# Four small edits to a one-core decoder block: later work on loads, a third row buffer, one low part on another engine, a moved constant

## The chip, the core and the metric

The kernel runs on one core of one Trainium2 chip. The metric is device time in microseconds (us) of one execution, the median over the runs shown. A profile of one further execution, taken by the hardware profiler, is read beside it.

## What is computed

One decoder layer on a sequence of 1024 tokens with 1024 channels, in float32:

```python
mod = silu(c) @ w_ada + b_ada
shift, scale, gate = split(mod, 3)
h = rms_norm(x, norm_gain) * (1 + scale) + shift
q, k, v, z_a, u, z_b, m_a, m_b = split(h @ w_in, ...)          # each (1024, 1024)
attn = stick_breaking_attention(q, k, v)                       # 16 heads of 64
p_a = (attn * silu(z_a)) @ w_branch_a
p_b = (multiscale_causal_pool(u, pool_w, pool_scale) * silu(z_b)) @ w_branch_b
out = (sigmoid(m_a) * p_a + sigmoid(m_b) * p_b) @ w_out
return rms_norm(x + gate * out, final_gain)
```

In the attention each weight is sigmoid(z) times the product of (1 - sigmoid(z)) over the keys between, under a strictly causal mask. The pooling takes means over trailing windows of 2, 4, 8 and 16 tokens, one window for each quarter of the channels.

## The kernel before, in words

**Split products.** Every large product is made of three matmuls in a reduced float32 format. A weight or an activation is held as a high part (a rounded copy, made by ScalarE or VectorE) and a low part (the value minus its high part, made by VectorE or GpSimd), and high x high, high x low and low x high are summed in PSUM (`mm3`, L162). `split` (L110) makes both parts, the high one at L119 or L123 and the low one at L114; `load_w` (L125) loads a tile of 128 x 1024 weights and calls it. The engines that make the two parts are its last arguments.

**Stages.** The work goes in this order: the modulation, the normalised input `hT` and the first half of u (up to L536); the second half of u (L571); the values v (L579 to L601); z_b with the pooled branch (L604 to L621); the product with w_branch_b (L630 to L641); attention together with the projections k, q, z_a, m_a, m_b (L649 to L940); and last the product with w_branch_a, the sum of the two branches, the product with w_out and the final norm (L943 to L1026).

**Low parts ahead of time.** The attention stage reads 40 tiles of `w_in` in the order of `tiles` (L131). The first `PLAIN` = 8 are split where they are loaded, by `load_parts` (L152): high part on ScalarE, low part on GpSimd. With index 0 the tile of the first pair's keys, 1 its queries, 2 its z_a, and 3 the second pair's keys, index 4 is the second pair's queries. For the 32 others `make_lo` (L138) runs in the earlier stages: it loads the tile (L147), makes the high part on ScalarE (L148), the low part on VectorE in place (L149), and stores it to DRAM in `wl_d` (L150). In the values' stage it has three buffers for the raw tile and one for the high part, and each step makes `LO_V[sb]` tiles, 0 or 1.

**Values' stage.** Two halves of eight steps. A step is 24 matmuls of 512 columns into one of two PSUM banks, a high part of the result on ScalarE (L593), a low part on VectorE (L594), a store (L595), then `make_lo`, and in steps 1, 4, 7 and 10 one `make_d` (L544), which loads a tile of u and computes window mean minus token on VectorE (L553 to L560). The weights of the second half of the stage are loaded and split in the same stage (`load_wv`, L565).

**Attention stage.** Its order on TensorE is written out and kept (`pinned`, L95): logits of blocks of 128 queries (L795), then two sigmoids on ScalarE into `om` and `be` (L797, L798), a mask on the diagonal block of each on GpSimd (L802), a running product on VectorE (L804), and a product of the two (L805), after which `om`, which has two buffers, is free. Later the weights are turned on TensorE with the identity `ident` as moving operand (L107), split again (L823, L824), and multiplied with the values (L835). Between these steps come pieces of the projections.

**Last stage.** For each half of the tokens and each of eight row blocks j, rows of sigmoid(m_a), sigmoid(m_b) and p_b are loaded from DRAM into `s_`, `m_` and `b_`, each with two buffers (L963 to L968). `m_` is multiplied with `b_` (L969), 24 matmuls `pa` run, VectorE multiplies the result by `s_` and frees the PSUM bank (L976), adds (L977), and splits the sum into `mhl` (L978, its low part at L114). These matmuls alternate in two PSUM banks with one another and lie among those of `o`, the product with w_out (L1000).

**What sets the order.** Outside the stretch that is pinned, the order of each engine's instructions is not the order of the program text: a planner that simulates a timeline sorts them, within the limits of the buffers. Each engine then executes its own list strictly in order, waiting where it must. Loads and stores are issued by SyncE's queue (SP), some stores by ScalarE's.

**Memory.** `const` holds the identity (512 bytes in each partition), a tile of ones of the same size, and small vectors; after it comes `big`, with `hT` and later `wo`, and then `wts`, the buffers for weights.

Of the kernel before, what the change touches and what calls it, by code (L numbers as in the profile page):

```python
# [9 lines left out]
F32 = mybir.dt.float32  # L10
F32R = mybir.dt.float32r
# [4 lines left out]
P = 128  # L16
# [18 lines left out]


PLAIN = 8
LO_V = (1, 0, 1, 1, 0, 1, 1, 0)
LO_ZB = (0, 1, 0, 1, 0, 1, 0, 1)
LO_PB = (1, 1, 1, 1, 1, 1, 2, 2)  # L40
# [9 lines left out]
WINDOWS = (2, 4, 8, 16)  # L50
# [5 lines left out]
def block_kernel(ctx, tc, a, out):  # L56
# [3 lines left out]
    def pool(name, **kw):  # L60
        return tc.tile_pool(name=name, bufs=1, reuse_waits="tile", **kw)

    const = ctx.enter_context(pool("const"))
    big = ctx.enter_context(pool("big"))
    wts = ctx.enter_context(pool("wts"))
    dram = ctx.enter_context(tc.tile_pool(name="dram", bufs=1, space=bass.MemoryType.DRAM))
    psp = ctx.enter_context(tc.tile_pool(name="psp", bufs=2, space=PSUM))
# [10 lines left out]
    u_d = dram.tile([KB, P, S], F32, name="u_d")  # L78
    wl_d = dram.tile([5 * KB, P, D], F32, name="wl_d")

    ident = const.tile([P, P], F32, name="ident")
    make_identity(nc, ident)
    ones = const.tile([P, P], F32, name="ones")
    gp.memset(ones, 1.0)
    mhalf = const.tile([P, 8], F32, name="mhalf")
    gp.memset(mhalf, -0.5)
# [48 lines left out]
    tiles += gates  # L135
    early_lo = iter(range(PLAIN, len(tiles)))

    def make_lo(pl, n, tag=None, bufs=3):  # L138

        for _ in range(n):  # L140
            i = next(early_lo)
            if tag:
                raw, hi = (pl.tile([P, D], t_, tag=tag, bufs=5, name=f"l{i}_{n_}") for n_, t_ in (("raw", F32), ("hi", F32R)))
            else:
                raw = pl.tile([P, D], F32, tag="lraw", bufs=bufs, name=f"l{i}_raw")
                hi = pl.tile([P, D], F32R, tag="lhi", bufs=1, name=f"l{i}_hi")
            nc.sync.dma_start(raw, a["w_in"][tiles[i]])  # L147
            act.copy(hi, raw)  # L148
            v.tensor_sub(raw.bitcast(F32R), raw, hi.bitcast(F32))  # L149
            nc.sync.dma_start(wl_d[i], raw)  # L150

    def load_parts(i, name):  # L152
        if i < PLAIN:
            return load_w(a["w_in"][tiles[i]], name, act, gp)
        raw = wts.tile([P, KB, P], F32, tag="raw", bufs=2, name=name + "_raw")
        nc.sync.dma_start(raw.rearrange("p k c -> p (k c)"), a["w_in"][tiles[i]])
        hl = wts.tile([P, 2, KB, P], F32R, tag="whl", bufs=2, name=name)
        nc.sync.dma_start(hl[:, 1].rearrange("p k c -> p (k c)").bitcast(F32), wl_d[i])
        act.copy(hl[:, 0], raw)
        return hl[:, 0], hl[:, 1]  # L160
# [380 lines left out]
        gp.memset(invn[:, j:j + 1], 1.0 / (16 - j))  # L541
    dhls = {}

    def make_d(j):  # L544
        win = WINDOWS[j // 2]
        u = dif.tile([P, S + 16], F32, tag="u", bufs=2, name=f"u{j}")
        v.memset(u[:, S:], 0.0)
        nc.sync.dma_start(u[:, :S], u_d[j])
        cur, n, step = u, S + 16, 1
        while step < win:  # L550
            nxt = dif.tile([P, S + 16], F32, tag="win", bufs=2, name=f"win{j}_{step}")
            n -= step
            v.tensor_add(nxt[:, :n], cur[:, :n], cur[:, step:step + n])  # L553
            cur, step = nxt, 2 * step
        t0 = S - win + 1
        d = dif.tile([P, S], F32, tag="d", bufs=5, name=f"d{j}")
        v.scalar_tensor_tensor(d[:, :t0], cur[:, :t0], 1.0 / win, u[:, :t0], ALU.mult, ALU.subtract)
        tl = dif.tile([P, 16], F32, tag="tl", bufs=2, name=f"tl{j}")
        v.tensor_mul(tl[:, :win - 1], cur[:, t0:S], invn[:, 16 - win + 1:])
        v.tensor_sub(d[:, t0:], tl[:, :win - 1], u[:, t0:S])  # L560
        dhls[j] = d


    with pool("vp") as vp:
        def load_wv(hf, k2):  # L565
            raw = wts.tile([P, 2, 512], F32, tag="raw", bufs=2, name=f"wv{hf}_{k2}_raw")
            nc.sync.dma_start(raw.rearrange("p k c -> p (k c)"), a["w_v"][hf, k2])
            return split(raw, [P, 2, 512], vp, "wv", 6, act, v, f"wv{hf}_{k2}")

        wv = [[load_wv(0, k2) for k2 in range(4)]]  # L570
        for i in reversed(range(KB)):  # L571
            ps = bank("pj", f"u{i}_1")
            mm3(ps, whl[i], h, range(KB), hmov(1))
            use[i](1, ps)
            make_lo(vp, 1)
        early.close()
        diffs = ExitStack()
        dif = diffs.enter_context(pool("dif", side="right"))
        for hf in range(2):  # L579
            if hf == 0:  # L580
                wv.append([load_wv(1, k2) for k2 in range(4)])
            for sb in range(8):
                ss = slice(sb * P, (sb + 1) * P)
                ps = bank("pj", f"v{sb}_{hf}")
                for kb in range(KB):
                    hh, hl = h_hi[:, kb, ss], h_lo[:, kb, ss]
                    wh, wl = (w[:, kb % 2] for w in wv[hf][kb // 2])
                    for n, (l, w) in enumerate(((hh, wh), (hh, wl), (hl, wh))):
                        mm(ps, l, w, start=kb == 0 and n == 0, stop=kb == KB - 1 and n == 2)

                vo = dif.tile([P, 8, 2, HD], F32R, tag="vo", bufs=3, name=f"vo{sb}_{hf}")
                pv = ps.rearrange("p (h d) -> p h d", d=HD)
                act.copy(vo[:, :, 0], pv)  # L593
                v.tensor_sub(vo[:, :, 1], pv, vo[:, :, 0].bitcast(F32))  # L594
                nc.sync.dma_start(  # L595
                    v_d[4 * hf:4 * hf + 4, :, sb].rearrange("n p c -> p n c"),
                    vo.rearrange("p (n h) i d -> p n (h i d)", h=2).bitcast(F32),
                )
                make_lo(vp, LO_V[sb])
                if 8 * hf + sb in DIFFS:  # L600
                    make_d(DIFFS[8 * hf + sb])  # L601


    with pool("pb") as pb:  # L604
        gb = pb.tile([P, 2, KB, S], F32R, name="gb")
        for j in range(KB):
            if j not in dhls:
                make_d(j)
            zs = [pb.tile([P, 512], F32, tag="zs", bufs=3, name=f"zs{j}_{sh}") for sh in range(2)]

            def silu(sh, ps):
                z, sl = zs[sh], slice(sh * 512, sh * 512 + 512)
                act.activation(z, ps, AF.Sigmoid)
                v.tensor_mul(z, ps, z)
                v.scalar_tensor_tensor(z, dhls[j][:, sl], psc_v[:, j:j + 1], z, ALU.mult, ALU.mult)
                act.copy(gb[:, 0, j, sl], z)
                v.tensor_sub(gb[:, 1, j, sl], z, gb[:, 0, j, sl].bitcast(F32))

            project(CZB + j, f"wzb{j}", silu, act, v)
            make_lo(pb, LO_ZB[j], bufs=2)  # L620
            del dhls[j]  # L621

        sg, gjunk = (dif.tile([P, S + 16], F32, tag="u", bufs=2, name=n)[:, :D] for n in ("sg", "gjunk"))
        nc.sync.dma_start(sg, a["c_row"].broadcast_to([P, D]))
        act.activation(gjunk, sg, AF.Sigmoid)
        v.tensor_mul(sg, sg, gjunk)
        gate = pb.tile([P, KB], F32, name="gate")
        bias = pb.tile([P, KB], F32, name="gbias")
        nc.sync.dma_start(bias, a["b_gate"])
        for j in range(KB):  # L630
            sm = [pb.tile([P, 512], F32, tag="zs", bufs=3, name=f"sm{j}_{sh}") for sh in range(2)]
            whl = load_w(a["w_branch_b"][j], f"wb{j}", v, gp)
            wg = wts.tile([P, D], F32, tag="raw", bufs=2, name=f"wg{j}")
            nc.sync.dma_start(wg, a["w_gate"][j])
            v.scalar_tensor_tensor(gjunk, wg, 1.0, sg, ALU.mult, ALU.mult, accum_out=gate[:, j:j + 1])
            for sh in range(2):
                ps = bank("pj", f"pb{j}_{sh}")
                mm3(ps, whl, (gb[:, 0], gb[:, 1]), range(KB), hmov(sh))
                act.copy(sm[sh], ps)
                nc.sync.dma_start(pb_d[j][:, sh * 512:sh * 512 + 512], sm[sh])  # L640
            make_lo(dif, LO_PB[j], "d")  # L641

        v.tensor_add(gate, gate, bias)
        nc.sync.dma_start(g_d[0].rearrange("(k p) -> p k", p=P), gate)
# [298 lines left out]
    with pool("fin") as fin:  # L943
# [14 lines left out]
        for sh in range(2):  # L958
            sl = slice(sh * 512, sh * 512 + 512)
            ms = []  # L960
            for j in range(KB):
                whl = load_w(a["w_branch_a"][j], f"wa{sh}_{j}", act, v)
                s_ = fin.tile([P, 512], F32, tag="s_", bufs=2, name=f"s{sh}_{j}")  # L963
                nc.sync.dma_start(s_, sa_d[j][:, sl])
                m_ = fin.tile([P, 512], F32, tag="m_", bufs=2, name=f"m{sh}_{j}")
                nc.sync.dma_start(m_, sb_d[j][:, sl])
                b_ = fin.tile([P, 512], F32, tag="b_", bufs=2, name=f"b{sh}_{j}")
                nc.sync.dma_start(b_, pb_d[j][:, sl])  # L968
                v.tensor_mul(m_, m_, b_)  # L969
                ps = bank("pj", f"pa{sh}_{j}")  # L970
# [111 lines left out]
```

## Time and profile before

| what | value |
|---|---|
| median of 3 runs | 1212.78 us (1212.56 to 1213.09) |
| the profiled execution's own time | 1212.4 us |
| span of its trace, first to last instruction | 1210.4 us |
| TensorE busy in the span | 1199.6 us, 99% |
| VectorE, ScalarE, GpSimd busy | 63%, 45%, 16% |
| mean granted TensorE clock | 0.999 of full speed |

PE is TensorE's matmuls, PEld its weight loads, DVE is VectorE, ACT is ScalarE, POOL is GpSimd, SP is SyncE; a q behind an engine's name means its queue, which issues transfers. Busy times of PE rest on modelled ends of matmuls, so that the distance between the starts of matmuls is a better measure of their pace than the duration of one.

### The profile page before, as it was taken

How to read it: one execution, taken by the hardware profiler on the slowest of the kernel's cores; microseconds unless marked ns; L12 is line 12 of the kernel's file. 1: busy time of each engine (PE TensorE's matmuls, PEld its weight loads, DVE VectorE, ACT ScalarE, POOL GpSimd, SP SyncE). 2: the span in 40 equal slices, each digit the busy share in tenths (PEclk: the TensorE clock that was granted, in tenths of full speed). 3: DMA queues.
4: the chain of work that ended last, by engine and by line, in shares of the span. 5: the costliest groups of instructions: out<-in, count | busy, mean ns of one | idle time of the engine just before them, and what ended most of it. 6: DMA issues, size and time to landing. Idle time of an engine off the chain costs nothing.

```text
span 1210.4 us, 16174 instructions
## 1 busy us (share of the span) xinstructions
PE 1199.6 (99%) x5746; PEld 1000.1 (83%) x5746; DVE 757.9 (63%) x1049; ACT 540.6 (45%) x1008; POOL 193.8 (16%) x361
## 2 busy tenths in 40 slices
PE   8999999999999999999999999999999999999997
PEld 7888888888888888888888888888888888888886
DVE  6764482677410277767768677776777763785643
ACT  5564341334211265665556655655655653232211
POOL 1000000001222343212212122231211310000001
PEclk9999999999999999999999999999999999999999
DMA  9649994626846632442635325353343236984622
GB/s 361 255 168 339 326 383 167 214 82 230 317 148 117 179 92 75 133 121 78 170 109 157 113 80 153 109 158 115 106 132 102 96 126 211 315 275 168 218 65 84
DMA packets 81955, 207.13 MB, mean 171 GB/s; under 512 B 10450, under 2 KB 23890, under 8 KB 79699
## 3 DMA queue, kind: packets, MB, share of 16 engines
q1 hardware_dynamic: 73666, 191.23, 49.2%
q10 hardware_dynamic: 8208, 14.88, 3.3%
q8 instruction: 45, 0.74, 0.2%
q14 instruction: 36, 0.29, 0.1%
HBM read 138.96 MB, written 50.34 MB: 156 GB/s over the span
## 4 chain that ended last, share of the span: by engine, by line
PE 93%; DVE 2%; DMA 2%; issue 1%; ACT 0%; POOL 0%; SPq 0%; POOLq 0%; DVEq 0%; ACTq 0%
PE p L99 36%; PE pb L99 7%; PE wzb L99 7%; PE v L99 7%; PE o L99 6%; PE av L99 6%; PE z L99 6%; PE wt L99 5%; PE pa L99 5%; PE u L99 5%; PE ua L99 3%; PE wm L99 1%; DMA m<-sb_d 1%; DMA out_y<-y 0%; DMA praw<-in_pool_w 0%
## 5 line engine op out<-in xcount | busy, mean ns | idle before, releaser
L99 PE MATMUL p<-hT,w 128*128 128x512 f32 x1920 | 480.9, 392 | 0.0
L99 PEld LDWEIGHTS p<-hT,w 128*128 128x128 f32 x1920 | 354.8, 188 | 68.6
L804 DVE TENSOR_TENSOR_SCAN om<-om 128x512 f32<-128x512 f32 (+7 forms) x128 | 175.4, 1370 | 50.0 <-ACT om L797 41.5
L824 DVE TENSOR_TENSOR wt<-wt,wt 128x512 fp32r<-128x512 f32 (+1 forms) x160 | 100.5, 628 | 93.7 <-ACT wt L823 93.1
L823 ACT CAST wt<-wt 128x512 fp32r<-128x512 f32 (+1 forms) x160 | 87.5, 547 | 130.2 <-PE wt L99 129.7
L797 ACT ACTIVATE om<-z 128x512 f32<-128x512 f32 (+2 forms) x192 | 94.9, 494 | 77.2 <-PE z L99 52.2
L802 POOL TENSOR_SCALAR_AFFINE_SELECT om<-om 128x128 f32<-128x128 f32 x128 | 50.9, 397 | 364.3 <-ACT om L797 344.0
L99 PE MATMUL av<-wt,vv 128*128 128x512 f32 x320 | 106.0, 412 | 0.0
L99 DVE TENSOR_TENSOR be<-be,om 128x511 f32<-128x511 f32 (+7 forms) x128 | 95.8, 758 | 0.3
L798 ACT ACTIVATE be<-z 128x512 f32<-128x512 f32 (+2 forms) x192 | 94.2, 491 | 0.0
L99 PE MATMUL pa<-ga,wa 128*128 128x512 f32 x384 | 89.9, 390 | 0.3 <-DVE s L976 0.2
L99 PEld LDWEIGHTS wt<-ident,be 128*128 128x128 f32 x576 | 72.7, 140 | 20.9
L99 PE MATMUL o<-wo,mhl 128*128 128x512 f32 (+1 forms) x408 | 89.6, 377 | 0.0
L99 PE MATMUL wt<-ident,be 128*128 128x128 f32 x576 | 88.7, 272 | 0.0
L99 PE MATMUL v<-wv,hT 128*128 128x512 f32 x384 | 87.2, 389 | 0.0
L99 PE MATMUL wzb<-hT,wzb 128*128 128x512 f32 x384 | 87.2, 389 | 0.0
L99 PE MATMUL pb<-gb,wb 128*128 128x512 f32 x384 | 87.2, 389 | 0.0
L99 PEld LDWEIGHTS o<-wo,mhl 128*128 128x128 f32 x408 | 73.5, 188 | 14.1
L99 PEld LDWEIGHTS pa<-ga,wa 128*128 128x128 f32 x384 | 71.9, 188 | 15.9 <-issue 0.6
L99 PEld LDWEIGHTS v<-wv,hT 128*128 128x128 f32 x384 | 72.1, 188 | 14.9
L99 PEld LDWEIGHTS wzb<-hT,wzb 128*128 128x128 f32 x384 | 72.1, 188 | 14.9
L99 PEld LDWEIGHTS pb<-gb,wb 128*128 128x128 f32 x384 | 72.1, 188 | 14.9
(129 smaller groups left out, 1374.2 us busy)
## 6 DMA issues: line engine op xcount, KB each, us to landing
w_raw<-in_w_in SPq DMA_DIRECT2D x40, 512.0 KB, 4.8
l_raw<-in_w_in SPq DMA_DIRECT2D x32, 512.0 KB, 5.1
wl_d<-l_raw SPq DMA_DIRECT2D x32, 512.0 KB, 5.8
w<-wl_d SPq DMA_DIRECT2D x32, 512.0 KB, 3.9
v_d<-vo SPq DMA_DIRECT2D x16, 512.0 KB, 4.8
vv<-v_d SPq DMA_DIRECT2D x8, 1024.0 KB, 5.5
wa_raw<-in_w_branch_a SPq DMA_DIRECT2D x16, 512.0 KB, 4.8
wa<-in_w_mod SPq DMA_DIRECT2D x7, 1024.0 KB, 6.5
```

The lines of the kernel that those rows point to most:

```text
L99: ins = op(*args, **kw)
L797: act.activation(om[:, b0:b0 + n], zp[:, :n], AF.Sigmoid, scale=-0.125)
L798: act.activation(be[:, b0:b0 + n], zp[:, :n], AF.Sigmoid, scale=0.125)
L802: gp.affine_select(out=tl[:, :P], in_=tl[:, :P], pattern=[[1, P]], compare_op=ALU.is_gt, fill=fill, base=0, channel_multiplier=-1)
L804: v.tensor_tensor_scan(om[:, :W], om[:, :W], om[:, :W], 1.0, ALU.mult, ALU.min)
L823: act.copy(wt[:, 0, :off], pt[:, :off])
L824: v.tensor_sub(wt[:, 1, :off], pt[:, :off], wt[:, 0, :off].bitcast(F32))
```

## The change

A tile of the values' stage that `make_lo` has loaded is worked on (high part, low part, store) one step later than it is loaded, and so is the computation of `make_d` behind its load of u. The low part of weight tile 4 of the attention stage moves from GpSimd to VectorE. `s_`, `m_` and `b_` get three buffers each. The identity and the ones move from `const` to a pool of their own behind `big`.

```diff
+MASKED = 4
...
     big = ctx.enter_context(pool("big"))
+    idp = ctx.enter_context(pool("idp"))
     wts = ctx.enter_context(pool("wts"))
...
-    ident = const.tile([P, P], F32, name="ident")
+    ident = idp.tile([P, P], F32, name="ident")
     make_identity(nc, ident)
-    ones = const.tile([P, P], F32, name="ones")
+    ones = idp.tile([P, P], F32, name="ones")
...
-    def make_lo(pl, n, tag=None, bufs=3):
+    def make_lo(pl, n, tag=None, bufs=3, later=False):
+        rest = []
         for _ in range(n):
...
             nc.sync.dma_start(raw, a["w_in"][tiles[i]])
-            act.copy(hi, raw)
-            v.tensor_sub(raw.bitcast(F32R), raw, hi.bitcast(F32))
-            nc.sync.dma_start(wl_d[i], raw)
+            def low(i=i, raw=raw, hi=hi):
+                act.copy(hi, raw)
+                v.tensor_sub(raw.bitcast(F32R), raw, hi.bitcast(F32))
+                nc.sync.dma_start(wl_d[i], raw)
+            if later:
+                rest.append(low)
+            else:
+                low()
+        return rest
...
-            return load_w(a["w_in"][tiles[i]], name, act, gp)
+            return load_w(a["w_in"][tiles[i]], name, act, v if i == MASKED else gp)
...
-    def make_d(j):
-        win = WINDOWS[j // 2]
+    def load_u(j):
         u = dif.tile([P, S + 16], F32, tag="u", bufs=2, name=f"u{j}")
         v.memset(u[:, S:], 0.0)
         nc.sync.dma_start(u[:, :S], u_d[j])
+        return u
+
+    def make_d(j, u):
+        win = WINDOWS[j // 2]
...
-                make_lo(vp, LO_V[sb])
+                now, todo = todo, make_lo(vp, LO_V[sb], later=True)
                 if 8 * hf + sb in DIFFS:
-                    make_d(DIFFS[8 * hf + sb])
+                    j = DIFFS[8 * hf + sb]
+                    todo.append(lambda j=j, u=load_u(j): make_d(j, u))
+                for f in now:
+                    f()
...
-                s_ = fin.tile([P, 512], F32, tag="s_", bufs=2, name=f"s{sh}_{j}")
+                s_ = fin.tile([P, 512], F32, tag="s_", bufs=3, name=f"s{sh}_{j}")
...
-                m_ = fin.tile([P, 512], F32, tag="m_", bufs=2, name=f"m{sh}_{j}")
+                m_ = fin.tile([P, 512], F32, tag="m_", bufs=3, name=f"m{sh}_{j}")
...
-                b_ = fin.tile([P, 512], F32, tag="b_", bufs=2, name=f"b{sh}_{j}")
+                b_ = fin.tile([P, 512], F32, tag="b_", bufs=3, name=f"b{sh}_{j}")
```

## Rows read from the trace of the kernel before

**Rows 1.** The page's first two parts: TensorE's busy time, and its granted clock in 40 slices.

```profile
PE 1199.6 (99%) x5746; PEld 1000.1 (83%) x5746; DVE 757.9 (63%) x1049; ACT 540.6 (45%) x1008; POOL 193.8 (16%) x361
...
PEclk9999999999999999999999999999999999999999
```

**Rows 2.** TensorE's waits over the span: total us, times, longest.

```profile
PE idle L99 <- POOL x L230: 1.6, 1, 1.6
...
PE z L99 <- ACT be L798: 0.4, 1, 0.4
PE pa L99 <- DVE s L976: 0.2, 1, 0.2
```

**Rows 3.** Busy time by stretches: us, PE, PEld, DVE, ACT, POOL, clock, DMA share, GB/s.

```profile
0.00:30.00 30.00, 26.16 (x118) 21.40 (x119) 18.07 (x33) 17.27 (x30) 4.37 (x32) 1.00 0.93 361
...
150.00:180.00 30.00, 30.00 (x134) 24.86 (x133) 25.85 (x33) 12.46 (x16) 0.00 (x0) 1.00 1.02 379
```

**Rows 4.** The chain that ended last, in order of time: start us, us, what.

```profile
79.84 48.47 PE u L99 x212
128.31 87.04 PE v L99 x384
215.35 87.04 PE wzb L99 x384
...
1102.37 21.77 PE o L99 x96
```

**Rows 5.** Timeline of the first masks: start us, us, engine, line, what, idle before.

```profile
425.42 1.23 POOL L802 TENSOR_SCALAR_AFFINE_SELECT be<-be 128x128 f32<-128x128 f32 x1
...
426.65 0.51 ACT L797 ACTIVATE om<-z 128x384 f32<-128x384 f32 x1
426.85 2.40 POOL L114 TENSOR_TENSOR w<-w_raw,w 128x1024 fp32r<-128x1024 f32 x1 [0.20 <-ACT w L119]
...
429.21 0.29 POOL L802 TENSOR_SCALAR_AFFINE_SELECT om<-om 128x128 f32<-128x128 f32 x1
...
429.53 1.02 DVE L804 TENSOR_TENSOR_SCAN om<-om 128x384 f32<-128x384 f32 x1 [2.39 <-POOL om L802]
...
430.46 1.54 PE L99 MATMUL p<-hT,w 128*128 128x512 f32 x6
431.25 0.60 ACT L797 ACTIVATE om<-z 128x512 f32<-128x512 f32 x1 [3.71 <-DVE be L99]
...
432.39 0.50 PE L99 MATMUL z<-kh,q 128*128 128x512 f32 x1 [0.38 <-ACT be L798]
...
439.60 0.59 ACT L692 CAST kh<-p 128x512 fp32r<-128x512 f32 x1 [1.16 <-PE p L99]
```

**Rows 6.** Instructions by line and shape: the same low part on VectorE in the last stage.

```profile
L114 DVE TENSOR_TENSOR wa<-wa_raw,wa 128x1024 fp32r<-128x1024 f32 x16 | 19.5, 1218 | 14.3 <-ACT wa L119 14.3
```

**Rows 7.** Timeline of the last stage, around the two waits of its matmuls.

```profile
1127.37 4.86 PEld L99 LDWEIGHTS pa<-ga,wa 128*128 128x128 f32 x22 [0.49 <-DVE wa L114]
...
1146.77 10.59 PE L99 MATMUL pa<-ga,wa 128*128 128x512 f32 x46
...
1153.03 0.32 SPq L966 DMA_DIRECT2D m<-sb_d  x1
1156.13 0.69 DVE L969 TENSOR_TENSOR m<-m,b 128x512 f32<-128x512 f32 x1 [3.12 <-DMA m<-sb_d]
1156.74 0.68 DVE L976 TENSOR_TENSOR s<-pa,s 128x512 f32<-128x512 f32 x1
...
1157.57 0.70 PE L99 MATMUL pa<-ga,wa 128*128 128x512 f32 x2 [0.21 <-DVE s L976]
```

**Rows 8.** Timeline of VectorE in the values' stage: a d, and the last low of wv.

```profile
153.84 1.23 DVE L553 TENSOR_TENSOR win<-win 128x1037 f32<-128x1037 f32 x1
...
156.12 1.22 DVE L557 SCALAR_TENSOR_TENSOR d<-win,u 128x1021 f32<-128x1021 f32 x1
...
172.06 1.22 DVE L114 TENSOR_TENSOR wv<-wv_raw,wv 128x1024 fp32r<-128x1024 f32 x1
```

More of the change, by code (lines that the diff above doesn't have):

```diff
@@ L577, in block_kernel @@
         diffs = ExitStack()
+        todo = []
         dif = diffs.enter_context(pool("dif", side="right"))
@@ L598, in block_kernel @@
                 )
-                make_lo(vp, LO_V[sb])
+                now, todo = todo, make_lo(vp, LO_V[sb], later=True)
                 if 8 * hf + sb in DIFFS:
-                    make_d(DIFFS[8 * hf + sb])
+                    j = DIFFS[8 * hf + sb]
+                    todo.append(lambda j=j, u=load_u(j): make_d(j, u))
+                for f in now:
+                    f()
+        assert not todo
     with pool("pb") as pb:
@@ L607, in block_kernel @@
             if j not in dhls:
-                make_d(j)
+                make_d(j, load_u(j))
             zs = [pb.tile([P, 512], F32, tag="zs", bufs=3, name=f"zs{j}_{sh}") for sh in range(2)]
```

## The prediction, made before the changed kernel was run

> **What bounds the kernel now.** I read the busy times first: TensorE is busy for 1199.6 of 1210.4 us, at its upper clock level, 2.4 GHz, in nearly every slice [rows 1]. So a part of the change can gain only where TensorE waits, and the next view is the list of its waits. Of six, the first and three more lie in the first stretch of 30 us, where it is busy for 26.16 us only [rows 2, 3]; no part of the change touches those. Two are left: 0.4 us at logits z, waiting for a sigmoid, and 0.2 us at pa, waiting for the step that frees a PSUM bank [rows 2].
>
> A modelled end hides part of a wait, so I measure pace by starts. The chain of waits gives it: 384 matmuls of v in 87.04 us and 384 of wzb in the same time are 0.2267 us each [rows 4]. The values' stage, where most lines of the change are, is then TensorE back to back from 128.31 to 215.35 us. That is the first thing to see: nothing can be gained there. For the two waits I use the timeline around each.
>
> **First masks, low part to VectorE.** Tile 4's low part runs on GpSimd for 2.40 us from 426.85 us. The mask of an `om` whose sigmoid began at 426.65 and took 0.51 us (ready at 427.16) has to queue behind it until 429.21; the running product on VectorE, idle for 2.39 us until then, starts at 429.53; `om` comes free and ScalarE goes on at 431.25; TensorE's next z starts at 432.39 [rows 5]. Six p started at 430.46 and would have been done at 430.46 + 6 x 0.2267 = 431.82. So 0.57 us are lost here.
>
> The change adds to VectorE one instruction of 1.22 us, the price of the same shape there [rows 6]. VectorE's gap runs from 427.14 to 429.53 [rows 5], and the high part ends just before 426.85, where GpSimd started on it, so the low part fits: 427.14 + 1.22 = 428.36. What then comes first decides the shift. If the mask runs beside it, the running product starts at 428.36, 1.17 us earlier; if the planner puts it before the low part, it can start about 427.5, 2.0 us earlier. Both cover 0.57. The weights have time: TensorE needs them after the second pair's keys, whose last copy starts at 439.60 [rows 5], some 10 us later. If VectorE's gap is not there because ScalarE or the planner has moved things, the low part costs at most its 1.22 us in that chain. I take -0.57.
>
> Here a row bears on the margin. A mask took 1.23 us beside a running product, where another takes 0.29 [rows 5]. The Trainium skill's SBUF — State Buffer, section Who interferes with whom, says that a VectorE instruction with two SBUF inputs and a GpSimd instruction that reads SBUF shut each other out, the second for the whole of the first. The trace agrees with it at that row (1.23 against 0.29 us). By that rule the mask would wait for the low part and the sum would still be -0.57, with a thinner margin. In numbers of the trace alone: a mask that starts at 428.36 and takes 0.29 lets the running product start about 428.7, 0.8 us earlier instead of 1.17, which leaves 0.26 over 0.57. One more delay of 0.3 us in that chain and part of the wait comes back; this is why I give the case without a gain below more than a token chance.
>
> What is late next? No wait of TensorE stands in the list between this one and the last stage, so up to 0.57 us of advance should be kept; a new wait of the same size is the other bound, 0.
>
> **Third buffers at the end.** 46 pa start at 1146.77 and end at 1146.77 + 46 x 0.2267 = 1157.20; the next start at 1157.57, 0.37 us late [rows 7]. The bank was freed by L976 at 1156.74, which stood on VectorE behind L969 at 1156.13, and that had idled for 3.12 us for the load of `m_`, issued at 1153.03 when its buffer came free [rows 7]. A third buffer frees the place one row block earlier, 24 x 0.2267 = 5.44 us, so that the load goes out about 1147.6 and lands about 1150.7; L969 then waits for nothing, and L976 follows 3 us earlier. -0.37. The other loss, 0.49 us at 1127.37, is a weight's low part (L114) [rows 7], which no buffer of rows touches; I leave it, as the bound below.
>
> The cost: 3 x 2 KB in each partition, and on SP the loads of `s_`, `m_`, `b_` may stand a block earlier, ahead of weight loads. Since their place is then free, they don't hold the queue longer; 0, at worst a slip like the 0.49 already there.
>
> **Values' stage.** Nothing is added or removed: each load, high part, low part, store and d has the same duration, a step (5.44 us) later. ScalarE and VectorE should wait less inside a step, which TensorE does not notice. On SP a step's store now stands behind the next step's load, and a raw buffer is held a step longer; three buffers against at most one tile a step allow it. The last tile's work falls under the first wzb, whose matmuls take 87.04 us without a gap [rows 4]. I take 0. What hides this work is slack on VectorE, and that is thin in one place: from 150 to 180 us it is busy for 25.85 of 30 us [rows 3]. More on that below.
>
> **Identity and ones.** No instruction more or less; `big` moves down by 1 KB. The trace can bound what a place is worth: v, wzb and o read operands in different places and run at 87.04/384 = 0.2267 and 21.77/96 = 0.2268 us [rows 4]. Some 3100 matmuls read `hT`; at 0.1 ns each that is 0.3 us either way. I take 0.
>
> **Sum.** -0.57 - 0.37 = -0.94 us. The profiled execution took 1212.4 us with a span of 1210.4, so it would be 1211.5; the median of the runs is 0.4 above it, 1212.78, so I forecast **1211.8**. About 0.2% (2.4 us) is what a measurement can tell from no change here, so this counts as none.
>
> **Rivals.**
> *More waits go* (0.17). Every edit lets the planner sort anew, and it may clear what I left: the 0.49 us at 1127, and in the second half of u 48.47 - 212 x 0.2267 = 0.41 us [rows 4]. With both, 1210.9; with 0.3 from the place, 1210.6. Past 1210.4 there is little in the trace after the first 30 us that could still be gained.
> *The change doesn't do what it says* (0.20). The planner sorts instructions outside the pinned stretch, so "a step later" may leave the order as it is, and one of the two waits may come back by the margins above. 1212.2 to 1212.8; for it speaks that the gap at the masks is a matter of tenths, against it that both waits are traced to the very instruction the change moves or frees.
> *VectorE becomes late in the values' stage* (0.13), the one that ends slower. The last low part of the second half's weights ends at 172.06 + 1.22 = 173.28 us [rows 8]. The second half starts at 128.31 + 192 x 0.2267 = 171.83 and needs that weight after 18 matmuls, at 175.9: 2.6 us of margin. Held work that now stands ahead of it costs 1.2 us for a low part, and for a d of window 4 two sums of 1.23, one of 1.22 and small ones, about 4.0 [rows 8]. One of each, 5.2, overruns by 2.6: 1214.4. Two d's and a low part, 9.2, by 6.6: 1218.4. It decides from 2.6 us ahead of that low part. For it speaks the busy VectorE of that stretch; against it, that the planner sees this due time.
>
> **Chances and range.** The forecast has 0.50, the rivals 0.17, 0.20 and 0.13. Faster by over 0.2% (under 1210.4) is a third of the first rival, 0.06; slower by over 0.2% (over 1215.2) most of the last, 0.10; within, 0.84. The range leaves out those tails: 1210.3, which takes in the low bounds, to 1214.0, which takes in no gain at all, the 1.22 us of a low part in the chain, and little of the last rival.
>
> **What would show it.** In the profile after: a DVE L114 `w` of about 1.22 us near 427 us and no POOL one there; the running product before 428.8; the p and z starts near 432 without a hole; seven POOL L114 `w` in place of eight. At the end: no idle of L969 for `m_` near 1156, and L976 right behind its pa. In the values' stage 384 v in 87.04 us as before; a higher number, or a wait of v for wv in TensorE's list, means the last rival. A changed pace of 0.2267, or transposes that take longer, would mean that the identity's place counts, and I would be wrong there. A time under 1210 would show that TensorE's lost time was more than these waits.

## The result, and the profile after

The changed kernel took 1216.22 us (median of 8 executions, 1215.54 to 1217.81), the kernel before 1212.92 (median of 8 in the same session, 1212.18 to 1214.39). The ratio is 1.0029, interval 1.0019 to 1.004: slower by 3.3 us, outside the forecast range, whose upper end was 1214.0. The profiled execution took 1215.54 us with a span of 1213.7, so 3.3 us more span than before.

The change moved line numbers: the matmul helper is now L103 (L99 before), the low part L118 (L114), the high part on ScalarE L123 (L119), the product with `s_` L998 (L976), the sum L999 (L977), the scaling of y L1041 (L1019).

The page's busy time and clock, to be held against [rows 1]:

```profile
PE 1199.5 (99%) x5746; PEld 999.7 (82%) x5746; DVE 759.9 (63%) x1050; ACT 541.8 (45%) x1008; POOL 194.3 (16%) x360
...
PEclk9999999999999999999999999999999999999999
```

TensorE is busy for the same time, at the same clock level, 2.4 GHz. So most of the 3.3 us are waiting, and the list of TensorE's waits says where (total us, times, longest):

```profile
PE pa L103 <- DVE wa L118: 3.7, 2, 2.2
PE idle L103 <- POOL x L243: 1.6, 1, 1.6
PE ua L103 <- ACT hT L103: 1.1, 1, 1.1
PE ua L103 <- DVE wg L103: 1.0, 1, 1.0
PE wm L103 <- DMA praw<-in_pool_w: 0.7, 1, 0.7
```

Against [rows 2] the two waits that the prediction worked on, z on `be` and pa on `s`, are gone. In their place stand two of pa for the low part of a weight tile, longest 2.2 us. The busy times by stretch show where (us, PE, PEld, DVE, ACT, POOL, clock, DMA share, GB/s), the first two rows answering to [rows 3]:

```profile
0.00:30.00 30.00, 25.65 (x118) 20.89 (x119) 17.99 (x33) 17.30 (x30) 4.38 (x32) 1.00 0.93 357
150.00:180.00 30.00, 30.00 (x134) 24.85 (x133) 25.74 (x33) 11.53 (x14) 0.00 (x0) 1.00 1.00 363
420.00:450.00 30.00, 30.00 (x149) 25.14 (x148) 25.49 (x29) 17.87 (x36) 10.20 (x17) 1.00 0.32 79
1020.00:1050.00 30.00, 28.54 (x126) 23.30 (x125) 14.39 (x20) 6.34 (x7) 0.00 (x0) 1.00 0.87 317
1110.00:1140.00 30.00, 27.76 (x123) 22.65 (x122) 15.21 (x23) 5.93 (x11) 1.92 (x4) 1.00 0.47 166
```

The values' stage and the first masks are full; two stretches of the last stage are not. The chain says the same of the pace (start us, us, what), against [rows 4]:

```profile
128.40 87.04 PE v L103 x384
215.44 87.04 PE wzb L103 x384
...
1103.77 21.76 PE o L103 x96
```

**The first hole.** Timelines of ScalarE, VectorE and TensorE near 1046 (start us, us, engine, line, what, idle before):

```profile
1040.57 1.05 ACT L123 CAST wa<-wa_raw 128x1024 fp32r<-128x1024 f32 x1 [5.25 <-DMA wa_raw<-in_w_branch_a]
...
1043.51 0.69 DVE L118 TENSOR_TENSOR mhl<-m,mhl 128x512 fp32r<-128x512 f32 x1
1045.14 0.69 DVE L998 TENSOR_TENSOR s<-pa,s 128x512 f32<-128x512 f32 x1 [0.95 <-PE pa L103]
1045.75 1.22 DVE L118 TENSOR_TENSOR wa<-wa_raw,wa 128x1024 fp32r<-128x1024 f32 x1
...
1047.02 2.35 PE L103 MATMUL pa<-ga,wa 128*128 128x512 f32 x9 [1.46 <-DVE wa L118]
```

The high part of tile 3 is ready at 1041.62, and VectorE is idle from about 1044.2. It does not make the low part, since its next entry is the product with `s_` of row block 2, which needs the pa that TensorE finishes only at 1045.1. Behind it the low part comes too late: the matmuls start 1.851 us apart instead of 0.227, a loss of 1.62. Before, the same low part ran at 1043.05, ahead of that product:

```profile
1043.05 1.22 DVE L114 TENSOR_TENSOR wa<-wa_raw,wa 128x1024 fp32r<-128x1024 f32 x1
...
1050.54 0.68 DVE L976 TENSOR_TENSOR s<-pa,s 128x512 f32<-128x512 f32 x1
```

**The second hole**, near 1130, in the same views:

```profile
1126.98 1.03 ACT L123 CAST wa<-wa_raw 128x1024 fp32r<-128x1024 f32 x1
...
1127.43 0.69 DVE L999 TENSOR_TENSOR m<-m,s 128x512 f32<-128x512 f32 x1
1128.56 1.42 DVE L1041 SCALAR_TENSOR_TENSOR y<-y,qq,fg 128x512 f32<-128x512 f32 x2 [0.44 <-POOL qq L1036]
1129.89 1.22 DVE L118 TENSOR_TENSOR wa<-wa_raw,wa 128x1024 fp32r<-128x1024 f32 x1
...
1131.17 5.76 PE L103 MATMUL pa<-ga,wa 128*128 128x512 f32 x24 [2.24 <-DVE wa L118]
```

The high part is ready at 1128.01; the two scalings of the fourth y, for which VectorE even waits 0.44 us, stand ahead. The starts lie 2.625 us apart: 2.40 lost. Before, the scalings stood behind that low part:

```profile
1126.10 1.22 DVE L114 TENSOR_TENSOR wa<-wa_raw,wa 128x1024 fp32r<-128x1024 f32 x1
...
1129.97 1.41 DVE L1019 SCALAR_TENSOR_TENSOR y<-y,qq,fg 128x512 f32<-128x512 f32 x2
```

The kernel before lost something at this tile too: its matmuls start 0.457 us apart there, 0.23 too many, waiting for the same low part. So the second hole adds 2.17.

**The balance.** By starts, 1.62 + 2.17 are added, and 0.54 at 432 (0.770 between two matmuls before, instead of 0.227) and 0.37 at 1157 are gone: +2.88. When v starts, 0.09 had been lost (128.40 against 128.31). The rest is no wait at all. TensorE needs longer for the same matmuls of the attention stage, as two pairs of rows of the chain show (before, then after; start us, us, what):

```profile
435.29 2.08 PE p L99 x9
...
1028.93 21.76 PE pa L99 x96
```

```profile
434.70 2.06 PE p L103 x9
...
1028.79 16.33 PE pa L103 x72
```

That is 593.64 us between them before and 594.09 after, 0.45 more, spread over some 3000 matmuls. The sum is then +3.42, against +3.36 measured in the span (1213.746 less 1210.382); the 0.06 left are small differences beside the waits. Which edit costs the 0.45 is shown with the experiments.

### The profile page after: what moved, and what is told of

It reads as the page before. It is cut to its first block, busy times and chain, and to the rows that moved or that the text cites. A ratio compares the mean times of both kernels' runs of the same rounds, so it can differ in the third digit from the quotient of the medians.

```text
span 1213.7 us, 16161 instructions
## 1 busy us (share of the span) xinstructions
PE 1199.5 (99%) x5746; PEld 999.7 (82%) x5746; DVE 759.9 (63%) x1050; ACT 541.8 (45%) x1008; POOL 194.3 (16%) x360
## 4 chain that ended last, share of the span: by engine, by line
PE 96%; DVE 1%; issue 1%; ACT 0%; DMA 0%; POOL 0%; SPq 0%; POOLq 0%; DVEq 0%; ACTq 0%
PE p L103 36%; PE wzb L103 7%; PE v L103 7%; PE pb L103 7%; PE pa L103 7%; PE o L103 6%; PE z L103 6%; PE av L103 6%; PE wt L103 5%; PE u L103 5%; PE ua L103 3%; PE wm L103 1%; DMA praw<-in_pool_w 0%; DVE wg L103 0%; DVE mj L103 0%
## 5 line engine op out<-in xcount | busy, mean ns | idle before, releaser
L103 PE MATMUL p<-hT,w 128*128 128x512 f32 x1920 | 481.2, 392 | 0.0
L103 PEld LDWEIGHTS p<-hT,w 128*128 128x128 f32 x1920 | 354.9, 188 | 68.8
L103 PE MATMUL av<-wt,vv 128*128 128x512 f32 x320 | 106.1, 413 | 0.0
L103 DVE TENSOR_TENSOR be<-be,om 128x511 f32<-128x511 f32 (+7 forms) x128 | 95.8, 758 | 0.3
L103 PE MATMUL pa<-ga,wa 128*128 128x512 f32 x384 | 89.9, 390 | 3.7 <-DVE wa L118 3.7
L103 PEld LDWEIGHTS wt<-ident,be 128*128 128x128 f32 x576 | 72.4, 139 | 21.0
L103 PE MATMUL o<-wo,mhl 128*128 128x512 f32 (+1 forms) x408 | 89.6, 377 | 0.0
L103 PE MATMUL wt<-ident,be 128*128 128x128 f32 x576 | 88.7, 271 | 0.0
L103 PEld LDWEIGHTS pa<-ga,wa 128*128 128x128 f32 x384 | 71.9, 188 | 19.5 <-DVE wa L118 4.5
L103 PE MATMUL v<-wv,hT 128*128 128x512 f32 x384 | 87.2, 389 | 0.0
L103 PE MATMUL wzb<-hT,wzb 128*128 128x512 f32 x384 | 87.2, 389 | 0.0
L103 PE MATMUL pb<-gb,wb 128*128 128x512 f32 x384 | 87.2, 389 | 0.0
L103 PEld LDWEIGHTS o<-wo,mhl 128*128 128x128 f32 x408 | 73.5, 188 | 14.1
L103 PEld LDWEIGHTS v<-wv,hT 128*128 128x128 f32 x384 | 72.1, 188 | 15.0
L103 PEld LDWEIGHTS wzb<-hT,wzb 128*128 128x128 f32 x384 | 72.1, 188 | 15.0
L103 PEld LDWEIGHTS pb<-gb,wb 128*128 128x128 f32 x384 | 72.1, 188 | 15.0
```

What stands on the lines that cost most here:

```text
L103: ins = op(*args, **kw)
```

## The experiments

Twelve kernels ran, each timed against the kernel before. Theory A in all of them: the planner, given third buffers, sorts VectorE's list anew and puts work that waits ahead of two low parts. Losses below are distances between the starts of neighbouring matmuls less 0.227 us.

**One part at a time.** Changed kernel with two buffers for the rows:

```diff
-                s_ = fin.tile([P, 512], F32, tag="s_", bufs=3, name=f"s{sh}_{j}")
+                s_ = fin.tile([P, 512], F32, tag="s_", bufs=2, name=f"s{sh}_{j}")
```

and the same for `m_` and `b_`.

> The changed kernel with two buffers again for the rows of the last stage; the other three parts stay. Theory A (the third buffers alone cost the time, by the order that VectorE's list gets in the last stage): both new waits of pa for a weight's low part (3.7 us in TensorE's waits) are gone and the 0.57 us at the first masks stay gained: 1212.9 - 0.6 = about 1212.3. Theory B (the later work in the values' stage or the moved identity costs it): the time stays within 1 us of 1216.2.

Measured: 1213.23 us, ratio 0.9998 (0.9989 to 1.0007). Both waits of pa are gone. The loss hangs on the third buffers. The 0.6 us that were to stay gained do not show in the time. The kernel before with only the third buffers (the opposite edit, in `s_`, `m_` and `b_`):

> The kernel before with three buffers for the rows of the last stage, nothing else. Theory A: the changed kernel's loss without its gain at the masks, 1212.9 + 3.3 + 0.6 = about 1216.8, with both waits of pa for a weight's low part and the 0.4 us wait of z as before. Theory B: no more than the 0.4 us that the forecast gave the third buffers, 1212.5.

Measured: 1216.79 us, ratio 1.0036 (1.0024 to 1.0049), and the same two losses, 1.62 at 1046 and 2.40 at 1130. Its waits:

```profile
PE pa L99 <- DVE wa L114: 3.7, 2, 2.2
...
PE z L99 <- ACT be L798: 0.4, 1, 0.4
```

The kernel before with only the moved low part:

```diff
-            return load_w(a["w_in"][tiles[i]], name, act, gp)
+            return load_w(a["w_in"][tiles[i]], name, act, v if i == 4 else gp)
```

> The kernel before with the low part of weight tile 4 on VectorE, nothing else. If the step of the forecast is right: z no longer waits for the sigmoid near 432 us, 0.57 us less, about 1212.3. The rival: VectorE's 1.2 us come back as a later wait and the time stays 1212.9.

Measured: 1213.22 us, ratio 1.0001 (0.9992 to 1.0009). The wait at z is gone, but in this profile TensorE waits in the values' stage, where that edit touches nothing:

```profile
PE v L99 <- DVE vo L594: 1.1, 2, 0.9
```

The gain of 0.54 us is seen in the trace and lost in such differences between executions. The identity and the ones moved alone (the same for `ones`, with the pool `idp`):

```diff
-    ident = const.tile([P, P], F32, name="ident")
+    ident = idp.tile([P, P], F32, name="ident")
```

> The kernel before with identity and ones in a pool behind the big one, nothing else. If places in SBUF don't count: 1212.9, and 384 v in 87.04 us, transposes at the same pace. The rival: a changed pace of transposes or of matmuls that read hT, by over 0.5 us in sum.

Measured: 1213.86 us, ratio 1.0008 (0.9999 to 1.0017): the time shows no effect clear of its interval. The trace does. From one and the same p behind the first masks (it starts at 432.96 in the trace of before) to the first pa, TensorE takes 596.26 us here and 595.81 in the kernel before. Over all fourteen traces it takes 595.79 to 595.81 in the four kernels without the moved identity and 596.23 to 596.26 in the ten with it, whatever else was edited. So the move costs 0.43 us or a little more. Most of it lies between matmuls that read `hT`, which the edit moves down by 1 KB; the transposes with the identity are no slower. Why the place counts was not tried.

And the values' stage worked a step later, alone:

```diff
-                make_lo(vp, LO_V[sb])
+                now, todo = todo, make_lo(vp, LO_V[sb], later=True)
...
+                for f in now:
+                    f()
```

> The kernel before with only the first edit, the values' stage's loads worked on a step later. The lists that the planner makes for the five engines are those of before, entry for entry, so theory A expects nothing: 1212.7 to 1213.3 and v in 87.04 us or, as in some profiles of unchanged values' stages, with up to 1.5 us of waits for vo. Rival: the edit alters what each instruction waits for and so has an effect of its own, 0.6 us or more either way.

Measured: 1212.55 us, ratio 0.9997 (0.9988 to 1.0006), and no wait of v in its list of waits. In the trace TensorE, ScalarE, GpSimd and SyncE's queue go through the same work in the same order as before, and so does VectorE but for one clearing of 0.07 us near 182; the edit changes the program text and next to nothing that an engine does.

**Is it the place on VectorE's list?** The changed kernel with three buffers, the load and both parts of the next weight tile written ahead of the product with `s_`, and that product kept behind:

```diff
-                whl = load_w(a["w_branch_a"][j], f"wa{sh}_{j}", act, v)
+                whl = load_wa(sh, j)[0] if j == 0 else ahead_[0]
...
-                v.tensor_mul(s_, ps, s_)
+                if j + 1 < KB:
+                    ahead_ = load_wa(sh, j + 1)
+                tc.keep_in_program_order(v.tensor_mul(s_, ps, s_))
```

(`load_wa` is `load_w` written out.)

> The changed kernel with its third buffers kept; only the place of one kind of work on VectorE is set by hand: the load and both parts of the next w_branch_a tile stand in the program ahead of this row block's product with s_ (L998), and L998 may not be moved ahead of that low part. Theory A (VectorE works its list strictly in order, and in the list planned with third buffers the work on rows and the scalings of y stand ahead of two low parts of weights): both waits of pa for a low part of wa, 1.6 us near 1046 and 2.4 us near 1130, are gone, and the time is 1216.2 - 3.7 to 4.0 = 1212.2 to 1212.5. Theory B (the third buffers let more loads of rows into the queue and they delay the weights themselves, whatever VectorE's list): rows stay ahead, a wait of 1 us or more stays at pa, the releaser then being ScalarE's high part or the load, and the time is 1214.5 or more.

Measured: 1214.77 us, ratio 1.0015 (1.0006 to 1.0023). Both waits for a low part of wa are gone, as A has it, yet the time lies 2.3 to 2.6 us above its figure, where B had put it; the wait that B asks for is not there. New waits, near 1091, have come in:

```profile
PE pa L103 <- ACT ga L785: 1.2, 1, 1.2
...
PE o L103 <- DVE wo L972: 0.3, 1, 0.3
```

By starts they cost 1.41 and 0.50 us. The first is for a piece of `ga` that ScalarE could start only when its load had landed; the planner had sorted more than the kept entries anew. The control with two buffers:

```diff
-                s_ = fin.tile([P, 512], F32, tag="s_", bufs=3, name=f"s{sh}_{j}")
+                s_ = fin.tile([P, 512], F32, tag="s_", bufs=2, name=f"s{sh}_{j}")
```

(and `m_`, `b_`, on top of the edit above).

> The same hand-set place, with two buffers for s_, m_ and b_. It is the control for the run with three: theory A expects the same time within 0.6 us, 1212.3 to 1213.0, so that the buffers by themselves are worth at most the 0.37 us for which the prediction wanted them. If the hand-set place itself cost something (low parts now ahead of products that free the PSUM bank), both kernels would show waits of pa for s, of up to 1.2 us each.

Measured: 1213.87 us, ratio 1.001 (1.0001 to 1.0019), 0.9 us above its expectation of 1213.0 at most: one wait for a low part of wa of 0.8 us near 1130 remains, and its profile also waits 1.0 us in u, which no edit touches. So an order set by hand costs something of its own, and the pair shows only that the two holes go when the order goes.

The low parts of w_branch_a on GpSimd:

```diff
-                whl = load_w(a["w_branch_a"][j], f"wa{sh}_{j}", act, v)
+                whl = load_w(a["w_branch_a"][j], f"wa{sh}_{j}", act, gp)
```

> The changed kernel with three buffers; the low parts of w_branch_a move from VectorE to GpSimd, which is nearly idle in the last stage, so that nothing on VectorE can stand ahead of them. A low part there takes about 2.45 us by the rows of the attention stage. Theory A: first hole gone (high part done at 1041.6, plus 2.45 = 1044.1, ahead of 1045.4); at the second the high part is done at 1128.0, so 1130.5 against 1128.8 leaves about 1.7 of 2.4: 1213.5 to 1214.5 in all. Theory B: the first hole stays at 1.6 us and the longer low part adds 1.2 to each: 1217.5 or more.

Measured: 1220.44 us, ratio 1.0069 (1.0056 to 1.0081). Both theories were wrong on the time: the largest wait is a new one, for `wo`. Its waits and the instruction behind the longest, with GpSimd's beside it:

```profile
PE o L103 <- ACT wo L971: 3.9, 2, 2.6
...
PE pa L103 <- POOL wa L118: 0.9, 1, 0.9
```

```profile
1081.11 2.47 POOL L118 TENSOR_TENSOR wa<-wa_raw,wa 128x1024 fp32r<-128x1024 f32 x1 [5.46 <-ACT wa L123]
...
1081.26 3.40 DVE L970 TENSOR_TENSOR wor<-wor,bg 128x1024 f32<-128x1024 f32 x1
```

VectorE's product for `wo` takes 3.40 us beside GpSimd's low part; the eight of them take 2.11 on the mean here and 1.22 in the changed kernel. By starts the waits for `wo` cost 2.80 and 1.42 us. Near 1046, 1.09 are still lost, but there the weight arrived later: its high part is ready at 1044.41, not at 1041.62, from which A's figure was worked out. The run tells nothing for or against A.

**Which buffer, and is each hole by itself?** The traces show that the two places move one by one with the choice of buffers. Third buffer for `m_` alone:

```diff
-                s_ = fin.tile([P, 512], F32, tag="s_", bufs=3, name=f"s{sh}_{j}")
+                s_ = fin.tile([P, 512], F32, tag="s_", bufs=2, name=f"s{sh}_{j}")
...
-                b_ = fin.tile([P, 512], F32, tag="b_", bufs=3, name=f"b{sh}_{j}")
+                b_ = fin.tile([P, 512], F32, tag="b_", bufs=2, name=f"b{sh}_{j}")
```

> The changed kernel with a third buffer for m_ alone, the one for which VectorE idled at 1156 before; s_ and b_ have two. The planner's list for VectorE then has the low part of tile wa0_3 ahead of the product with s_ of block 2 again. Theory A: no wait at 1046; near 1130 at most the wait as long as a scaling of y stands ahead; the wait at 1157 gone (0.37): 1212.2 to 1213.4. Theory B, by which more row loads in flight do the harm: a third of the 4.0 us at least stays, 1213.8 or more.

Measured: 1212.10 us, ratio 0.9995 (0.9986 to 1.0004), and no wait in the last stage at all. Third buffers for `s_` and `m_`:

```diff
-                b_ = fin.tile([P, 512], F32, tag="b_", bufs=3, name=f"b{sh}_{j}")
+                b_ = fin.tile([P, 512], F32, tag="b_", bufs=2, name=f"b{sh}_{j}")
```

> The changed kernel with third buffers for s_ and m_, two for b_. In the list that the planner makes for VectorE the first of the two places is as before (the low part of tile wa0_3 ahead of the product with s_ of block 2), the second is as in the changed kernel (sum and both scalings of the last y ahead of the low part of wa1_2). Theory A (each hole is made by the place of a low part on VectorE's list, and the two are independent): no wait near 1046, 2.4 us near 1130, so 1216.2 - 1.6 = 1214.6, with 0.6 either way. Theory B (the harm is that more loads of rows are in flight): two thirds of it, both holes present but shorter, 1214.9 at the end but with a hole near 1046.

Measured: 1216.42 us, ratio 1.0018 (1.001 to 1.0027). Only the second hole is there, with the same 2.40 us, so the trace bears A out; the time does not. Of its eleven executions three took 1213.9 to 1214.3, about as forecast, and eight 1216.0 to 1216.6; the profiled one is of the eight. What it shows is told in the last section. The counterpart, third buffers for `s_` and `b_`:

```diff
-                m_ = fin.tile([P, 512], F32, tag="m_", bufs=3, name=f"m{sh}_{j}")
+                m_ = fin.tile([P, 512], F32, tag="m_", bufs=2, name=f"m{sh}_{j}")
```

> The counterpart: third buffers for s_ and b_, two for m_. As many added buffers and as many bytes of them as in the run with s_ and m_; but on VectorE's list both low parts stand as before, wa0_3 ahead of the product with s_ of block 2, and wa1_2 ahead of the whole work on the last two y. Theory A: neither hole, the wait for m_ of 0.37 us near 1157 may be back: 1212.2 to 1213.3. Theory B: the same time as with s_ and m_, 1214.6 to 1215.

Measured: 1212.13 us, ratio 0.999 (0.9981 to 0.9999), neither hole, and no wait near 1157 although `m_` has two buffers. With as many added buffers and bytes as the run before it, it is 4 us faster. That takes theory B away as it was put: it is the order, not the number of loads in flight. Since the order of the loads on SP differs between the two as well, the pair alone does not say that it is VectorE's; the timelines of the two holes do, where VectorE leaves a low part lying whose input is ready, and so does the next run.

**One entry of the list.** Changed kernel, three buffers; only the scalings of the fourth y leave VectorE:

```diff
-                        v.scalar_tensor_tensor(y[:, cl], y[:, cl], q[:, 7:8], fg[:, cl], ALU.mult, ALU.mult)
+                        if sb == 3:
+                            act.mul(y[:, cl], y[:, cl], q[:, 7:8])
+                            gp.tensor_mul(y[:, cl], y[:, cl], fg[:, cl])
+                        else:
+                            v.scalar_tensor_tensor(y[:, cl], y[:, cl], q[:, 7:8], fg[:, cl], ALU.mult, ALU.mult)
```

> The changed kernel with its three buffers; of the fourth y alone, the scaling that stands on VectorE ahead of the low part of wa1_2 is made by ScalarE and GpSimd instead. The lists of the engines stay those of the changed kernel but for this entry and a few neighbours behind it. Theory A (the second hole is made by what stands ahead on VectorE's list): the low part of wa1_2 starts when the sum ahead of it ends, 1128.11 instead of 1129.89 in the times of the changed kernel's profile, so 1.8 of the 2.4 us go and some 0.6 stay, while the first hole of 1.6 near 1046 is as it was: 1216.2 - 1.8 = 1214.4, with 0.6 either way. Theory B (loads of rows or of the weight come late): high part or load of wa1_2 ends the wait and the hole stays at 2 us or more, 1215.9 or more. On the clock: with no stall of over 2 us left in the last stage, no matmul behind it should start at twice the usual distance (427 instead of 227 ns), as they did in the profiles with third buffers for s_ and m_ and with third buffers alone.

Measured: 1214.54 us, ratio 1.0014 (1.0005 to 1.0023), where A said 1214.4. VectorE and TensorE near 1130:

```profile
1128.34 0.69 DVE L999 TENSOR_TENSOR m<-m,s 128x512 f32<-128x512 f32 x1
1128.95 1.23 DVE L118 TENSOR_TENSOR wa<-wa_raw,wa 128x1024 fp32r<-128x1024 f32 x1
...
1130.24 5.29 PE L103 MATMUL pa<-ga,wa 128*128 128x512 f32 x22 [0.40 <-DVE wa L118]
```

The low part starts when the sum ends. The loss is 0.56 us (A: 0.6) in place of 2.40, and the first hole still loses 1.62. In the last stage no engine's order differs from that of the changed kernel ahead of 1129. The holes are separate, and the second is made by what stands ahead on VectorE.

The losses of the last stage together (only those of over 0.4 us; the run with low parts on GpSimd is left out, since its largest losses lie elsewhere):

| kernel | near 1046 | near 1130 | elsewhere | us | ratio |
|---|---|---|---|---|---|
| changed | 1.62 | 2.40 | none | 1216.22 | 1.0029 |
| before, only third buffers | 1.62 | 2.40 | none | 1216.79 | 1.0036 |
| third `s_`, `m_` | none | 2.40 | none | 1216.42 | 1.0018 |
| three, fourth y off VectorE | 1.62 | 0.56 | none | 1214.54 | 1.0014 |
| three, low part ahead by hand | none | none | 1.41, 0.50 | 1214.77 | 1.0015 |
| two, low part ahead by hand | none | 0.94 | none | 1213.87 | 1.0010 |
| two buffers | none | none | none | 1213.23 | 0.9998 |
| third `m_` | none | none | none | 1212.10 | 0.9995 |
| third `s_`, `b_` | none | none | none | 1212.13 | 0.9990 |

The last two versions beat the changed kernel by some 4 us. Against the kernel before, their medians are a tenth of a percent lower at most, and only the last interval leaves out 1, barely. The times of the second and third rows hold executions in which the second hole was paid for twice (last section).

## Why the prediction was wrong

*First masks, -0.57: right.* Timeline near 427, against [rows 5]:

```profile
426.74 0.52 ACT L819 ACTIVATE om<-z 128x384 f32<-128x384 f32 x1
...
427.14 1.22 DVE L118 TENSOR_TENSOR w<-w_raw,w 128x1024 fp32r<-128x1024 f32 x1
427.32 1.19 POOL L824 TENSOR_SCALAR_AFFINE_SELECT om<-om 128x128 f32<-128x128 f32 x1 [0.59 <-ACT om L819]
...
428.55 1.02 DVE L826 TENSOR_TENSOR_SCAN om<-om 128x384 f32<-128x384 f32 x1 [0.19 <-POOL om L824]
```

The low part stands exactly in the gap, 427.14 to 428.36. From the sigmoid to the running product it takes 1.81 us, before 2.88: 1.07 earlier, between the 1.17 and the 0.8 that the prediction weighed. The mask beside the low part takes 1.19 us, one that runs alone 0.29. The Trainium skill's SBUF — State Buffer, section Who interferes with whom, has a VectorE instruction with two SBUF inputs contend with a GpSimd instruction that reads SBUF, and the trace agrees with it here; it agrees again in the other direction, in the run with low parts on GpSimd, with VectorE's 3.40 against 1.22 us. The wait at 432 went, 0.54 by starts, in all ten kernels that have this edit, and stayed in the four that do not.

*Third buffers, the gain of -0.37: the wait is gone, but not shown to be the buffers' doing, and not in the way that was forecast.* VectorE still idles for `m_`, 1.53 us instead of 3.12, where the prediction had it wait for nothing. It is the order that changed: the product with `s_` now stands ahead of the product with `m_` and waits for its pa alone:

```profile
1155.10 0.69 DVE L998 TENSOR_TENSOR s<-pa,s 128x512 f32<-128x512 f32 x1 [0.48 <-PE pa L103]
1157.32 0.69 DVE L991 TENSOR_TENSOR m<-m,b 128x512 f32<-128x512 f32 x1 [1.53 <-DMA m<-sb_d]
```

And the wait at 1157 is missing as well in the profiles of four kernels that have two buffers and the last stage of before: the changed kernel with two buffers, the low part alone, the identity alone, and the step later alone. VectorE idles there for `m_` as it did before, 3.0 to 3.2 us, and the product still comes in time. The low part alone (VectorE and TensorE):

```profile
1156.47 0.69 DVE L969 TENSOR_TENSOR m<-m,b 128x512 f32<-128x512 f32 x1 [3.17 <-DMA m<-sb_d]
...
1147.95 11.04 PE L99 MATMUL pa<-ga,wa 128*128 128x512 f32 x48
```

So the 0.37 us was a wait that the one profile of before happened to have. That the changed kernel's profile lacks it is no evidence for the third buffers.

*Third buffers, the cost: the step that failed.* It said that loads of rows may stand a block earlier, ahead of weight loads, and put this at "0, at worst a slip like the 0.49 already there". It looked at SP's queue alone. VectorE's order changed as well: with the third buffers alone it is that of before up to 1043 us and another one from there on. The planner put a product that waits for TensorE, and two scalings that wait for GpSimd, ahead of low parts, and on an engine that goes through its list in order they hold up a low part whose input is ready. (By what rule the planner chose so was not looked into; that rows which can arrive sooner let it place the work on rows sooner is a guess.) The two holes lose 1.62 + 2.40 = 4.02 us, 3.79 more than the 0.23 that the kernel before lost at the second place. The bound was too small: the 0.49 us [rows 7] is the same wait, of the same matmuls for the same tile's low part (0.49 is the idle time of the weight loads; by starts the matmuls lost 0.23), and what could be queued ahead of such low parts stood just behind them in the timeline of before, at 1050.54 and 1129.97, and was never added up.

*Values' stage, 0: right.* v takes 87.04 us as before; alone, the edit is not told from no change. "A step later" did not change the order, as the second rival had it for this part.

*Identity, 0: wrong by a small term.* The pace of v, wzb and o is unchanged, but the attention stage takes 0.43 us longer with the moved identity. That is above the prediction's own bound of 0.3 either way and takes back most of what the masks gained, so that even without the third buffers hardly anything was left to win. The prediction had named such a change of pace as a sign of being wrong; the time alone would not have shown it.

*The rivals.* The slower one named the right mechanism, VectorE late with a low part of a weight, and its 1214.4 to 1218.4 us hold the result. It put it in the values' stage, where the list did not change, and not in the last one, where the edit gave the planner new freedom. That the result lies within its two figures is therefore luck.

## What to carry to other kernels

Where a planner sorts the work, a larger buffer is a change of order, not only of when a load may start: look, on each engine that runs in order, at what may now stand ahead of the instruction that the bottleneck waits for, and add up that work and its own waits. Try such freedom one buffer at a time: a third one for `m_` alone, or for `s_` and `b_`, opened no hole, one for `s_` and `m_` opened one, all three opened two. Before a short wait is credited to an edit, look for it in profiles of kernels that leave that place as it was; here it came and went by itself. Losses and gains of half a microsecond were not to be told apart in these times, even where the traces agreed on them to some hundredths.

## What had not been expected of the hardware

**The clock after a stall.** The profile with third buffers for `s_` and `m_` has the same wait of 2.24 us as the changed kernel, and then 24 matmuls that take 7.36 us, where the changed kernel has 5.76. The matmuls of that profile, and its busy times by 2 us (columns as above):

```profile
1129.73 7.36 PE L103 MATMUL pa<-ga,wa 128*128 128x512 f32 x24 [2.24 <-DVE wa L118]
```

```profile
1128.00:1130.00 2.00, 0.27 (x1) 0.28 (x2) 2.00 (x4) 0.12 (x1) 0.00 (x0) 1.00 0.88 327
1130.00:1132.00 2.00, 2.00 (x8) 1.54 (x8) 2.00 (x4) 0.00 (x0) 0.00 (x0) 0.73 0.70 175
1132.00:1134.00 2.00, 2.00 (x6) 1.54 (x5) 1.93 (x4) 0.00 (x0) 0.00 (x0) 0.50 0.85 291
1134.00:1136.00 2.00, 2.00 (x9) 1.64 (x8) 0.13 (x1) 0.00 (x0) 0.00 (x0) 0.92 0.69 239
```

The same stretch in the changed kernel:

```profile
1132.00:1134.00 2.00, 2.00 (x10) 1.66 (x9) 2.00 (x4) 0.00 (x0) 0.00 (x0) 1.00 0.77 246
```

With third buffers for `s_` and `m_` the granted clock of that stretch is 0.50, the lower level, 1.2 GHz, after TensorE had stood still for 2.24 us; seven matmuls start 0.427 us apart instead of 0.227, and in all some 1.6 us are lost. The profile of the kernel before with only the third buffers shows it too (six matmuls at that distance behind the second hole), the changed kernel's does not. So a stall can be paid for a second time in some executions, which is the likely reason for the two groups of times above. The mean granted clock, recorded for each execution, fits: 0.998 in all of the eight and 0.999 in the three; and of the changed kernel and of the one with only third buffers the two longest executions each have 0.998 (1217.06 and 1217.81, 1218.05 and 1219.35 us), the others more. It is no proof, since kernels without a hole have 0.998 in some executions that are no longer than the rest. What decides it is open: behind the longest stall of all, the 2.64 us for `wo` in the run with low parts on GpSimd, the profile shows 1.00, as it does behind the first hole (1.46 us) and behind the 0.40 us that were left in the last run.

**Waits that come and go.** Kernels with the same order in the values' stage waited there for `vo` between nothing and 1.1 us, with DMA busy throughout (a share of 1.00 in the rows for 150 to 180 us). The profile with third buffers for `s_` and `b_` waits 1.1 us in pb, which no edit touches either. What decides it was not tried.
